# Expert outputs by way of DRAM rows for five of sixteen pairs, and three weight loads under way instead of two

## The chip, the cores and the metric

The program runs on one core of a Trainium2 chip. The metric is the device time of one execution in microseconds. The kernel before takes 706.75 us (median of three runs, 706.09 to 708.14). All engine names are those of the profile: PE is the matrix engine and PEld its weight loads, DVE, ACT and POOL are the vector, scalar and general engines, and SP only issues DMAs.

## The reference

One decoder layer on 512 tokens of width 1024, all in float32: RMSNorm, two attention branches with gates, an output projection, and then a mixture of experts with a final RMSNorm. What matters here is the mixture:

```python
g_sel = argmax(hf @ w_rg + b_rg)                  # one of 4 groups for each token
top_vals, top_idx = top_k(logits of the 8 experts in that group, 2)
weight = p_group * softmax(top_vals)
expert_id = g_sel * 8 + top_idx                    # two of 32 experts for each token
y[slot] = (silu(xs @ w_g[e]) * (xs @ w_u[e])) @ w_d[e]
out[token] += y[slot] * weight[slot]               # the sum of two slots for each token
```

The weights of each expert are three matrices of 1 MB, 96 MB for all 32, and every expert's weights are read once.

## The kernel before

The first 435 us hold the attention branches and the output projection. Each of those steps splits its operands in a high and a low part, and x2[0] to x2[3], four tiles of 128 tokens by 1024, hold the residual stream at their end. A router (class Route) then finds two experts for each token and its place among the tokens of that expert.

The experts are worked off in 16 pairs, q from 0 to 15, in `experts` (L819). A pair takes 128 slots, 64 for each of its two experts. One pair goes through these steps, in this order on PE:

- `gate_up` (L760): 32 matmuls G and 32 matmuls U (L769). ACT makes silu of G with the slots' norm factor (L774), DVE multiplies it with U (L775). The result is `a`.
- `some(5)`: five of the eight units of `combine` (L811) that the pair before has left. A unit is two matmuls of 128x512 (L815, L816) with a one-hot matrix S of slots against tokens, and one DVE addition to x2 (L817). There are 8 units in a pair: 4 token tiles by 2 halves of the width.
- `act_T` (L778): two transposes of `a` (L781) and a copy on ACT (L783).
- `some(3)`: the other three units.
- `next_rows`: eight transposes (L746) of the rows xg, which were gathered for the next pair.
- `down` (L786): 16 matmuls yp (L795), and for each half of the width a multiplication by the slots' weights sw on ACT (L802) and a low part on DVE (L803), both into the tile yhl. These are what the next pair's combine units multiply with S.

`gather_rows` (L723) is called at the end of pair q for pair q+2: two indirect DMAs on POOL fetch 128 rows of x2 (xg, from x2d) and of the routing weights (wg, from Wd). `slot_weights` (L733), three small copies on POOL at the top of each pair, makes sw and the norm factor out of wg.

PE and POOL keep the order in which the program states their work (`manual_schedule`, L826). The order on DVE, ACT and SP is the planner's. The pools that matter: mp has four PSUM buffers, which the combine units and the transposes share, yp has two, wg two, and xg, S, a and yhl one each.

The weights come in loads of 1 MB, 6 for each pair, all issued on SP by `load` (L678), which lets a load start when the load two before it has landed (L680, L681). There are NH = 20 buffers for them (`new_w`, L669), so a load also waits until the load 20 before it has been used. Pairs 0 to 2 are asked for ahead of the loop, pair q+2 at the top of pair q. The last pair's down weights come as four loads of 512 KB.

`last` (L876) is the combination of pair 15 and the final norm. The rows of x2 that leave the kernel take their additions from all pairs, so all combine units and the additions of the new way must be done before it ends.

Of the kernel before, what the change touches and what calls it, by code (L numbers as in the profile page):

```python
# [10 lines left out]
F32 = mybir.dt.float32  # L11
# [3 lines left out]
I32 = mybir.dt.int32  # L15
U32 = mybir.dt.uint32
AF = mybir.ActivationFunctionType
ALU = mybir.AluOpType
# [3 lines left out]
P = 128  # L22
T = 512
NT = T // P
D = 1024
# [5 lines left out]
NEG = -1e30  # L31
NE = 32
NH = 20


class Layer:
# [593 lines left out]
    def route_setup(self):  # L630
        nc, tc, io, c = self.nc, self.tc, self.io, self.const
        self.dram = dp = self.ctx.enter_context(tc.tile_pool(name="dram", bufs=1, space=bass.MemoryType.DRAM))
        self.x2d = dp.tile([T, D], F32, name="x2d")
        self.Wd = dp.tile([T, NE + 1], F32, name="Wd")
        self.wr = c.tile([P, KD, 40], F32, name="wr")
        nc.gpsimd.memset(self.wr, 0.0)
        self.load_late(self.wr[:, :, 0:4], io["w_router_group"][0].rearrange("(j p) g -> p j g", p=P))
        for g in range(4):
            self.load_late(self.wr[:, :, 8 + 8 * g:16 + 8 * g],
                              io["w_router_expert"][0, g].rearrange("(j p) e -> p j e", p=P))  # L640
        self.gpj = c.tile([P, KD], F32, name="gpj")
        self.load_late(self.gpj, io["ffn_norm"][0].rearrange("(p j) -> p j", p=P))
        self.gcol = gcol = c.tile([P, KD], F32, name="gcol")
        self.load_late(gcol, io["ffn_norm"][0].rearrange("(j p) -> p j", p=P))
        nc.vector.tensor_scalar(self.gpj, self.gpj, 32.0, None, ALU.mult)
        nc.vector.tensor_scalar(gcol, gcol, 32.0, None, ALU.mult)
        nc.vector.tensor_tensor(self.wr, self.wr, gcol.unsqueeze(2).to_broadcast([P, KD, 40]), ALU.mult)
        self.rb = c.tile([P, 40], F32, name="rb")
        nc.gpsimd.memset(self.rb, -3e38)
        self.load_late(self.rb[:, 0:4], io["b_router_group"][0:1, :].to_broadcast([P, 4]))  # L650
        self.load_late(self.rb[:, 8:40], io["b_router_expert"].rearrange("o g e -> o (g e)")
                          .to_broadcast([P, 32]))
        self.rc = c.tile([P, 33 + NT], F32, name="rc")
        self.load_late(self.rc, io["rconst"])
        self.iota32 = self.rc[:, 0:32]
        self.slot = self.rc[:, 32:33]
        self.token = self.rc[:, 33:33 + NT]
        self.tri = c.tile([P, 2, P], F16, name="tri")
        self.after(nc.gpsimd.dma_start(self.tri, io["tri"]), self.started)
        self.tm = c.tile([P, T], F16, name="tm")  # L660
        self.after(nc.gpsimd.dma_start(self.tm, io["tm"]), self.started)
        self.M = c.tile([P, NT, NE], F16, name="M")
        self.sq = c.tile([P, 2, NT], F32, name="sq")
        self.W = c.tile([P, NT, NE + 1], F32, name="W")
        self.iotaU = c.tile([P, NE], U32, name="iotaU")
        nc.vector.tensor_copy(self.iotaU, self.iota32)
# [10 lines left out]

    def load(self, dst, src):  # L678
        d = self.nc.sync.dma_start(dst, src)
        if len(self.loads) >= 2:  # L680
            self.after(d, self.loads[-2])  # L681
        self.loads.append(d)

    def load_w(self, src, how):
# [126 lines left out]
    def combine(self, S, y, half, t):  # L811
# [4 lines left out]
        nc.tensor.matmul(cp, S[:, t * P:(t + 1) * P], y[1], start=False, stop=True)  # L816
        nc.vector.tensor_tensor(self.x2[t][:, hs], self.x2[t][:, hs], cp, ALU.add)  # L817

    def experts(self):  # L819
        nc, tc = self.nc, self.tc  # L820
        NP = NE // 2
        wgu, wd = {}, {}
        for q in range(3):
            wgu[q], wd[q] = self.load_gu(q), self.load_d(q)
        self.yhl = self.wp.tile([P, 2048], F32R, name="yhl", tag="whi")
        with tc.manual_schedule(engines={mybir.EngineType.PE, mybir.EngineType.Pool}):  # L826
            xT, sw, xg = {0: self.xT0}, {}, {}
            S, y, todo = None, None, []
            for q in range(NP):
                if q > 0 and q + 2 < NP:  # L830
                    wgu[q + 2], wd[q + 2] = self.load_gu(q + 2), self.load_d(q + 2)
                    if q + 2 == NP - 1:
                        self.load_final()
                if q:
                    sw[q] = self.slot_weights(q, wg, nc.gpsimd)

                def some(n):
                    for _ in range(min(n, len(todo))):
                        self.combine(S, y[todo[0][0]], *todo[0])
                        todo.pop(0)  # L840

                def between(j):
                    if q == 0 and j == 3:
                        self.tokens()
                        xg[1] = self.gather_rows(self.xi[:, 1:2], self.rows)
                    if q == 0 and j == 5:
                        sw[0] = self.take_weights()
                    if q == 0 and j == 9:
                        self.count_blocks()
                a = self.gate_up(wgu.pop(q), xT.pop(q), lambda: sw[q][1], between)  # L850
                def next_rows():
                    xT[q + 1] = self.new_xT()
                    for g in range(2):
                        self.gathered_T(xg[q + 1][0], xT[q + 1], g)
                if q == 0:
                    next_rows()
                some(5)
                aT = self.act_T(*a)
                some(3)
                if 0 < q < NP - 1:  # L860
                    next_rows()
                if q + 1 < NP:
                    wg = xg.pop(q + 1)[1]
                if q + 2 < NP:
                    xg[q + 2] = self.gather_rows(self.xi[:, q + 2:q + 3])
                S = self.one_hot(self.xf[:, q:q + 1])
                dn = wd.pop(q)
                y = [None, None]
                todo = [(h, t) for h in range(2) for t in range(NT)]
                if q == NP - 1:  # L870
                    self.last(S, dn, aT, sw[q][0])
                    break
                for h in range(2):
                    y[h] = self.down(dn, aT, sw[q][0], h)
# [158 lines left out]
class Route:  # L1033
# [60 lines left out]
    def choose_experts(self):  # L1094
        nc, L = self.nc, self.L
        self.v8, vi = self.tmp("v8", [8]), self.tmp("vi", [8], U32)
        nc.vector.max(self.v8, self.es)
        nc.vector.max_index(vi, self.v8, self.es)
        self.Mk = self.tmp("Mk", [2, NE])
        nc.vector.tensor_tensor(self.Mk, L.iotaU.unsqueeze(1).to_broadcast([P, 2, NE]),  # L1100
                                vi[:, 0:2].unsqueeze(2).to_broadcast([P, 2, NE]), ALU.is_equal)
        nc.vector.tensor_tensor(L.M[:, self.t], self.Mk[:, 0], self.Mk[:, 1], ALU.add)
# [15 lines left out]

    def places(self):
        nc, L, t, N = self.nc, self.L, self.t, self.N  # L1120
        n = self.tmp("n", [2])
        for c in range(2):
            nc.vector.scalar_tensor_tensor(self.es, self.Mk[:, c], 1.0, N, ALU.mult, ALU.mult, accum_out=n[:, c:c + 1])
        self.at(self.AB[:, :, 0:64], n)
# [33 lines left out]
def shape_consts():  # L1158
    out = {}

    def tab(half):
        e = (-np.arange(half, dtype=np.float32) / np.float32(half)).astype(np.float32)
        inv = np.power(np.float32(500000.0), e).astype(np.float32)
        ang = np.arange(T, dtype=np.float32)[:, None] * inv[None, :]
        c, s = np.cos(ang).astype(np.float32), np.sin(ang).astype(np.float32)
        return [c, c, -s, s]
    out["rope"] = np.ascontiguousarray(np.concatenate(tab(16) + tab(8), axis=1))
    q = np.arange(P)[:, None]
    c = np.arange(T)[None, :]
    out["mask"] = np.where(c <= q + 384, np.float32(0), np.float32(NEG)).astype(np.float32)  # L1170
    tri = np.ones((P, 2, P), np.float32)
    tri[:, 0] = np.arange(P)[:, None] <= np.arange(P)[None, :]
    tri[:, 0] += 1024.0 * np.eye(P)
    out["tri"] = tri
    rc = np.zeros((P, 33 + NT), np.float32)
    rc[:, 0:32] = np.arange(32)
    rc[:, 32] = 1025 + np.arange(P) % 64
    rc[:, 33:] = np.arange(P)[:, None] + P * np.arange(NT)[None, :] - 1024
    out["rconst"] = rc
    out["tm"] = np.broadcast_to(np.arange(T, dtype=np.float32) - 1024, (P, T)).copy()  # L1180
    return out
# [30 lines left out]
```

## Time and profile before

| | us |
|---|---|
| median of three runs | 706.75 |
| the profiled execution's own time | 705.33 |
| its span | 703.5 |
| PE busy | 683.6 (97%) |
| DVE busy | 398.8 (57%) |
| ACT busy | 277.3 (39%) |
| POOL busy | 70.9 (10%) |

The span runs from the first to the last instruction. A row of the page's second part cuts it in 40 slices of 17.6 us, each digit being the busy share in tenths. Busy shares leave out DMA issues. An arrow in square brackets at a row's end names what ended the idle time ahead of it on its engine.

### The profile page before, as it was taken

Reading aid. Unit: us, or ns where it says so; the run is one execution under the profiler, and the core shown is the slowest. Engines: PE = TensorE matmul, PEld = TensorE weight load, DVE = VectorE, ACT = ScalarE, POOL = GpSimd, SP = SyncE. Lnnn points to the kernel's source line nnn. Section 1 sums busy time; section 2 is a strip of 40 time slices with the busy share of each in tenths; the row PEclk is TensorE's granted clock in tenths of the full one; section 3 lists DMA queues with packets and bytes.
Section 4 is the critical chain, followed back from the end, with each engine's and each line's share of the span. In section 5 each row is a group of like instructions: output and inputs, shape, how many; then the busy total and the mean of one; then the engine's idle time right before and its main releaser. Section 6 shows DMA issues by size and latency. Waiting matters only on the chain.

```text
span 703.5 us, 11377 instructions
## 1 busy us (share of the span) xinstructions
PE 683.6 (97%) x4262; PEld 522.5 (74%) x4262; DVE 398.8 (57%) x972; ACT 277.3 (39%) x623; POOL 70.9 (10%) x151
## 2 busy tenths in 40 slices
PE   8999999999999999999999999999999999999991
PEld 7998887777788888888888998566656666666651
DVE  5535956877829964423765317255555544555545
ACT  5747544555638663422333334211212111212123
POOL 1404000000000000000000012211121111111103
PEclk9999999999999999999999999999999999999996
DMA  8725431110272144212789758898999999999923
GB/s 256 152 61 90 106 121 60 61 49 13 68 171 61 27 156 119 61 61 94 262 301 352 287 189 315 316 361 308 377 364 393 392 394 355 372 377 348 367 89 122
DMA packets 73786, 148.17 MB, mean 211 GB/s; under 512 B 30938, under 2 KB 53554, under 8 KB 61952
## 3 DMA queue, kind: packets, MB, share of 16 engines
q1 hardware_dynamic: 67616, 138.69, 56.1%
q10 hardware_dynamic: 3040, 4.27, 2.3%
q0 software_dynamic: 3072, 4.46, 2.1%
q8 instruction: 35, 0.57, 0.3%
q14 instruction: 23, 0.19, 0.1%
HBM read 145.35 MB, written 4.26 MB: 213 GB/s over the span
## 4 chain that ended last, share of the span: by engine, by line
PE 88%; DMA 4%; issue 3%; DVE 2%; ACT 1%; POOL 1%; SPq 0%; POOLq 0%; DVEq 0%; ACTq 0%
PE yp L795 7%; PE G L769 6%; PE U L769 6%; PE pacc L96 5%; PE pacc L95 5%; PE pacc L94 5%; PE pacc L448 4%; PE pacc L447 4%; PE pacc L449 4%; PE cp L815 4%; PE cp L816 3%; PE ptr L420 3%; DMA wg<-Wd,xi 3%; PE S L402 2%; PE O L428 2%
## 5 line engine op out<-in xcount | busy, mean ns | idle before, releaser
L65 DVE SCALAR_TENSOR_TENSOR wlo<-wraw,ms,whi 128x256 fp32r<-128x256 f32 (+2 forms) x134 | 68.3, 552 | 31.4 <-ACT whi L64 31.2
L64 ACT ACTIVATE whi<-wraw,ms 128x256 fp32r<-128x256 f32 (+2 forms) x134 | 67.0, 559 | 42.1 <-PE pacc L448 20.1
L817 DVE TENSOR_TENSOR x<-x,cp 128x512 f32<-128x512 f32 x128 | 78.1, 682 | 0.8 <-PE cp L816 0.8
L94 PE MATMUL pacc<-whi,hThi 128*128 128x352 f32 (+1 forms) x192 | 72.6, 378 | 0.0
L95 PE MATMUL pacc<-wlo,hThi 128*128 128x352 f32 (+1 forms) x192 | 70.6, 369 | 0.0
L96 PE MATMUL pacc<-whi,hTlo 128*128 128x352 f32 (+1 forms) x192 | 70.5, 367 | 0.0
L775 DVE SCALAR_TENSOR_TENSOR a<-U,sw,a 128x256 f32<-128x256 f32 x16 | 11.0, 685 | 84.9 <-PE U L769 62.0
L795 PE MATMUL yp<-w,a 128*64 128x512 f32 x256 | 58.5, 598 | 0.5 <-ACT a L783 0.5
L769 PE MATMUL G<-w,xT 128*64 128x256 f32 x512 | 58.3, 380 | 0.0
L769 PE MATMUL U<-w,xT 128*64 128x256 f32 x512 | 58.2, 379 | 0.0
L769 PEld LDWEIGHTS G<-w,xT 128*64 128x64 f32 x512 | 36.5, 137 | 24.6 <-issue 4.6
L815 PE MATMUL cp<-yhl,S 128*128 128x512 f32 x128 | 53.6, 419 | 0.2 <-DVE x L817 0.2
L816 PE MATMUL cp<-yhl,S 128*128 128x512 f32 x128 | 50.8, 396 | 0.8 <-DVE yhl L803 0.8
L447 PE MATMUL pacc<-hThi,whi 128*128 128x512 f32 x128 | 50.6, 396 | 0.0
L448 PE MATMUL pacc<-hTlo,whi 128*128 128x512 f32 x128 | 50.4, 394 | 0.0
L769 PEld LDWEIGHTS U<-w,xT 128*64 128x64 f32 x512 | 36.7, 137 | 18.4
L449 PE MATMUL pacc<-hThi,wlo 128*128 128x512 f32 x128 | 50.1, 392 | 0.0
L415 ACT ACTIVATE E<-E,mx 128x128 f32<-128x128 f32 (+3 forms) x64 | 35.6, 557 | 20.5 <-DVE mx L412 19.7
L803 DVE SCALAR_TENSOR_TENSOR yhl<-yp,sw,yhl 128x512 fp32r<-128x512 f32 x32 | 24.0, 751 | 31.3 <-ACT yhl L802 31.3
L802 ACT ACTIVATE yhl<-yp,sw 128x512 fp32r<-128x512 f32 x32 | 22.0, 687 | 47.4 <-PE yp L795 47.4
L94 PEld LDWEIGHTS pacc<-whi,hThi 128*128 128x128 f32 x192 | 36.1, 188 | 5.2 <-issue 1.3
L95 PEld LDWEIGHTS pacc<-wlo,hThi 128*128 128x128 f32 x192 | 36.1, 188 | 4.5 <-issue 0.7
(221 smaller groups left out, 1307.8 us busy)
## 6 DMA issues: line engine op xcount, KB each, us to landing
w<-in_w_exp_gate_dram SPq DMA_DIRECT2D x32, 1024.0 KB, 6.1
w<-in_w_exp_up_dram SPq DMA_DIRECT2D x32, 1024.0 KB, 6.1
w<-in_w_exp_down_dram SPq DMA_DIRECT2D x30, 1024.0 KB, 5.8
wraw<-in_w_in_dram SPq DMA_DIRECT2D x14, 1024.0 KB, 5.3
wraw<-in_w_out_dram SPq DMA_DIRECT2D x4, 1024.0 KB, 7.1
wraw<-in_w_in_dram SPq DMA_DIRECT2D x5, 704.0 KB, 4.8
xs<-in_x_dram SPq DMA_DIRECT2D x4, 512.0 KB, 6.6
wraw<-in_w_o_mla_dram SPq DMA_DIRECT2D x4, 512.0 KB, 3.4
```

Source lines behind the costliest of these rows:

```text
L65: nc.vector.scalar_tensor_tensor(lo[:, k], raw[:, k], g, hi[:, k].bitcast(F32), ALU.mult, ALU.subtract)
L94: nc.tensor.matmul(ps[t][:, :ncols], act_hi[kk // 4][:, kk % 4, ts], hi[:, k], start=kk == 0, stop=False)
L95: nc.tensor.matmul(ps[t][:, :ncols], act_hi[kk // 4][:, kk % 4, ts], lo[:, k], start=False, stop=False)
L96: nc.tensor.matmul(ps[t][:, :ncols], act_lo[kk // 4][:, kk % 4, ts], hi[:, k], start=False, stop=kk == ktot - 1)
L447: nc.tensor.matmul(ps, hi[:, k, ds], self.hT[0][k // 4][:, k % 4], start=k == 0, stop=False)
L448: nc.tensor.matmul(ps, hi[:, k, ds], self.hT[1][k // 4][:, k % 4], start=False, stop=False)
L449: nc.tensor.matmul(ps, lo[:, k, ds], self.hT[0][k // 4][:, k % 4], start=False, stop=k == KD - 1)
L769: nc.tensor.matmul(GU[i][es, 0:256], xT[:, j, es], gu[e][i][:, j * 256:(j + 1) * 256], start=j == 0, stop=j == KD - 1)
L795: nc.tensor.matmul(yp[es], aT[:, j, es], wd[e][:, j * D + half * 512:j * D + half * 512 + 512], start=j == 0, stop=j == 1)
L815: nc.tensor.matmul(cp, S[:, t * P:(t + 1) * P], y[0], start=True, stop=False)
L816: nc.tensor.matmul(cp, S[:, t * P:(t + 1) * P], y[1], start=False, stop=True)
L817: nc.vector.tensor_tensor(self.x2[t][:, hs], self.x2[t][:, hs], cp, ALU.add)
```

## The change

For the pairs in VIA = (1, 3, 5, 7, 9), the slots' outputs are no longer combined by matmuls. `down_out` multiplies the two halves by sw on ACT into one tile y of 128x1024, and ACT issues a DMA that writes it to rows of a DRAM tensor yd (640 rows of 4 KB). In pairs 11 to 14, `take_slots` is called twice for token tile t = q - 11, once for each of a token's two choices: POOL clears a tile y, an indirect DMA on POOL fetches for each token the row yd[yi], where an index out of bounds fetches nothing, and DVE adds the tile to x2[t]. The indices yi are worked out in pair 1 (`slot_rows`) from the router's choices (Mk) and places (place), which are now kept, and from a constant row `base`.

The combine units of the pairs that are left are spread: in pairs 1 to 10 two units stand ahead of `act_T` and two behind it, so the eight units of pair 0, 2, 4, 6 and 8 last for two pairs. From pair 11 on it is five and three again, as before.

Thirdly, `load` waits for the load three before instead of two before.

```diff
+VIA = (1, 3, 5, 7, 9)
+        self.yd = dp.tile([len(VIA) * P, D], F32, name="yd")
...
     def load(self, dst, src):
         d = self.nc.sync.dma_start(dst, src)
-        if len(self.loads) >= 2:
-            self.after(d, self.loads[-2])
+        if len(self.loads) >= 3:
+            self.after(d, self.loads[-3])
...
+    def slot_rows(self):
+        nc, c = self.nc, self.const
+        rows = c.tile([P, NT, 2], F32, name="yrows")
+        far = c.tile([P, NT, 2], F32, name="far")
+        junk = c.tile([P, NE], F32, name="yjunk")
+        for t in range(NT):
+            for i in range(2):
+                nc.vector.scalar_tensor_tensor(junk, self.Mk[:, t, i], 1.0, self.base, ALU.mult, ALU.mult,
+                                               accum_out=rows[:, t, i:i + 1])
+        nc.vector.tensor_scalar(far, self.place, 1088.5, float(1 << 20), ALU.is_gt, ALU.mult)
+        nc.vector.tensor_tensor(rows, rows, self.place, ALU.add)
+        self.yi = c.tile([P, NT, 2], I32, name="yi")
+        nc.vector.tensor_tensor(self.yi, rows, far, ALU.add)
+
+    def down_out(self, wd, aT, sw, q):
+        nc = self.nc
+        y = self.bl.tile([P, D], F32, name="y", tag="yd", bufs=2)
+        for h in range(2):
+            nc.scalar.mul(y[:, h * 512:h * 512 + 512], self.down_products(wd, aT, h), sw)
+        i = VIA.index(q) * P
+        nc.scalar.dma_start(self.yd[i:i + P], y)
+
+    def take_slots(self, t, i):
+        nc = self.nc
+        y = self.bl.tile([P, D], F32, name="y", tag="yd", bufs=2)
+        nc.gpsimd.memset(y, 0.0)
+        nc.gpsimd.indirect_dma_start(out=y, out_offset=None, in_=self.yd,
+                                     in_offset=bass.IndirectOffsetOnAxis(ap=self.yi[:, t, i:i + 1], axis=0),
+                                     bounds_check=len(VIA) * P - 1, oob_is_err=False)
+        nc.vector.tensor_tensor(self.x2[t], self.x2[t], y, ALU.add)
...
-                some(5)
+                n = min(len(todo), 4) if VIA[0] <= q <= VIA[-1] + 1 else len(todo)
+                some((n + 1) // 2 + (n > 4))
                 aT = self.act_T(*a)
-                some(3)
+                some(n // 2 - (n > 4))
...
                 if q + 2 < NP:
                     xg[q + 2] = self.gather_rows(self.xi[:, q + 2:q + 3])
+                if q == 1:
+                    self.slot_rows()
+                if 0 <= q - VIA[-1] - 2 < NT:
+                    for i in range(2):
+                        self.take_slots(q - VIA[-1] - 2, i)
+                dn = wd.pop(q)
+                if q in VIA:
+                    self.down_out(dn, aT, sw[q][0], q)
+                    continue
                 S = self.one_hot(self.xf[:, q:q + 1])
-                dn = wd.pop(q)
```

The rest of the diff keeps Mk and place in tiles of their own and lengthens the constant rc by the 32 columns of `base`.

## Rows read from the trace of the kernel before

**Rows 1.** The page, its second part: busy tenths of the DMA engines and the rate of the DMAs, in 40 slices of the span.
```profile
DMA  8725431110272144212789758898999999999923
GB/s 256 152 61 90 106 121 60 61 49 13 68 171 61 27 156 119 61 61 94 262 301 352 287 189 315 316 361 308 377 364 393 392 394 355 372 377 348 367 89 122
```
**Rows 2.** What PE waited for from 435 us to the end, all of it: us in total, times, the longest.
```profile
PE yp L795 <- ACT a L783: 0.5, 1, 0.5
PE cp L816 <- DVE yhl L803: 0.8, 1, 0.8
PE cp L815 <- DVE x L817: 0.2, 1, 0.2
```
**Rows 3.** PE's instructions in order of time, of pair 2, the start of pairs 3 and 4 and the down products of pair 5: start, length, form, count. Of the units' matmuls, the second and third unit's first ones.
```profile
465.55 3.62 PE L769 MATMUL G<-w,xT 128*64 128x256 f32 x32
...
473.12 0.39 PE L815 MATMUL cp<-yhl,S 128*128 128x512 f32 x1
...
473.59 0.39 PE L815 MATMUL cp<-yhl,S 128*128 128x512 f32 x1
...
477.70 3.65 PE L795 MATMUL yp<-w,a 128*64 128x512 f32 x16
481.19 3.62 PE L769 MATMUL G<-w,xT 128*64 128x256 f32 x32
...
497.56 3.62 PE L769 MATMUL G<-w,xT 128*64 128x256 f32 x32
...
525.48 3.65 PE L795 MATMUL yp<-w,a 128*64 128x512 f32 x16
```
**Rows 4.** The same view, of pair 15: its gate and its down products.
```profile
669.86 3.62 PE L769 MATMUL G<-w,xT 128*64 128x256 f32 x32
...
681.02 3.65 PE L795 MATMUL yp<-w,a 128*64 128x512 f32 x16
```
**Rows 5.** SP's issues in order of time: start, time from the first issue's start to the last one's end, tile and source, count. The gate rows are those of pair 3, 4 and 15, the up and down rows at 440 and 447 us those of pair 3.
```profile
429.40 3.46 SPq L679 DMA_DIRECT2D w<-in_w_exp_gate_dram  x2
440.87 1.15 SPq L679 DMA_DIRECT2D w<-in_w_exp_up_dram  x2
447.23 3.29 SPq L679 DMA_DIRECT2D w<-in_w_exp_down_dram  x2
453.52 3.59 SPq L679 DMA_DIRECT2D w<-in_w_exp_gate_dram  x2
...
504.63 2.82 SPq L679 DMA_DIRECT2D w<-in_w_exp_down_dram  x2
509.63 2.83 SPq L679 DMA_DIRECT2D w<-in_w_exp_gate_dram  x2
...
651.30 2.82 SPq L679 DMA_DIRECT2D w<-in_w_exp_gate_dram  x2
...
669.33 0.55 SPq L679 DMA_DIRECT2D w<-in_w_exp_down_dram  x1
```
**Rows 6.** From the view of the tile w in the window from 669 to 670 us: the time from the last load's issue to its landing.
```profile
DMA to landing us min/median/max: 6.0/6.0/6.0
```
**Rows 7.** Busy time by windows; the last three columns are the granted clock of PE, the busy share of the 16 DMA engines and GB/s. The windows are a stretch without gathers, the stretch from gate 4 to the last up load, and the last 10.5 us of the loads.
```profile
504.63:514.66 10.03, 10.03 (x57) 6.12 (x58) 7.77 (x14) 2.67 (x6) 2.24 (x3) 1.00 1.01 408
...
453.50:664.80 211.30, 211.09 (x1428) 132.47 (x1425) 110.78 (x188) 41.26 (x80) 34.35 (x68) 1.00 0.96 369
664.80:675.30 10.50, 10.50 (x79) 6.11 (x79) 4.91 (x9) 3.58 (x6) 0.00 (x0) 1.00 0.68 229
```
**Rows 8.** The DMA view from 453 to 675 us: the queue of POOL's gathers with packets, MB and share of the engines' time, and the row gathers with their count and median us from issue to landing.
```profile
q0 software_dynamic: 2288, 3.66, 4.7%
...
xg<-x2d,xi POOLq DMA_INDIRECT x13, 6.9
```
**Rows 9.** POOL's instructions in order of time, end of pair 5 (gathers for pair 7) and the first two copies of pair 6; ahead of them a clearing of a 128x1024 tile, and the copy of pair 3, which waited longest.
```profile
429.26 0.95 POOL L619 MEMSET xg<- 128x1024 f32 x1
...
487.97 0.18 POOL L738 COPY sw<-wg 64x1 f32<-64x1 f32 x1 [7.38 <-DMA wg<-Wd,xi]
...
525.83 1.02 POOL L728 DMA_INDIRECT xg<-x2d,xi  x1 [6.81 <-PE ptr L746]
527.15 1.03 POOL L728 DMA_INDIRECT wg<-Wd,xi  x1 [0.30 <-issue]
528.17 0.20 POOL L738 COPY sw<-wg 64x1 f32<-64x1 f32 x1
533.08 0.18 POOL L738 COPY sw<-wg 64x1 f32<-64x1 f32 x1 [4.70 <-DMA wg<-Wd,xi]
```
**Rows 10.** ACT and DVE in order of time, in pair 6.
```profile
533.54 0.72 ACT L774 ACTIVATE a<-G,sw 128x256 f32<-128x256 f32 x1 [3.58 <-POOL sw L739]
...
536.17 0.68 DVE L775 SCALAR_TENSOR_TENSOR a<-U,sw,a 128x256 f32<-128x256 f32 x1 [5.43 <-PE U L769]
536.74 4.87 DVE L817 TENSOR_TENSOR x<-x,cp 128x512 f32<-128x512 f32 x8
```
**Rows 11.** What SP waited for over the whole span: us in total, times, the longest.
```profile
SPq L679 <- DMA w<-in_w_exp_gate_dram: 87.9, 28, 8.7
...
SPq L679 <- PE cp L816: 3.0, 12, 0.3
```
**Rows 12.** DVE in the tail: a two-input operation on a 128x1024 tile.
```profile
691.58 1.28 DVE L922 SCALAR_TENSOR_TENSOR fin<-x,rstd,fin 128x1024 f32<-128x1024 f32 x1 [0.58 <-POOL rstd L915]
```

More of the change, by code (lines that the diff above doesn't have):

```diff
@@ L652, in route_setup @@
                           .to_broadcast([P, 32]))
-        self.rc = c.tile([P, 33 + NT], F32, name="rc")
+        self.rc = c.tile([P, 33 + NT + NE], F32, name="rc")
         self.load_late(self.rc, io["rconst"])
@@ L657, in route_setup @@
         self.token = self.rc[:, 33:33 + NT]
+        self.base = self.rc[:, 33 + NT:]
         self.tri = c.tile([P, 2, P], F16, name="tri")
@@ L662, in route_setup @@
         self.M = c.tile([P, NT, NE], F16, name="M")
+        self.Mk = c.tile([P, NT, 2, NE], F32, name="Mk")
+        self.place = c.tile([P, NT, 2], F32, name="place")
         self.sq = c.tile([P, 2, NT], F32, name="sq")
@@ L1098, in choose_experts @@
         nc.vector.max_index(vi, self.v8, self.es)
-        self.Mk = self.tmp("Mk", [2, NE])
+        self.Mk = L.Mk[:, self.t]
         nc.vector.tensor_tensor(self.Mk, L.iotaU.unsqueeze(1).to_broadcast([P, 2, NE]),
@@ L1120, in places @@
         nc, L, t, N = self.nc, self.L, self.t, self.N
-        n = self.tmp("n", [2])
+        n = L.place[:, t]
         for c in range(2):
@@ L1174, in shape_consts @@
     out["tri"] = tri
-    rc = np.zeros((P, 33 + NT), np.float32)
+    rc = np.zeros((P, 33 + NT + NE), np.float32)
     rc[:, 0:32] = np.arange(32)
     rc[:, 32] = 1025 + np.arange(P) % 64
-    rc[:, 33:] = np.arange(P)[:, None] + P * np.arange(NT)[None, :] - 1024
+    rc[:, 33 + NT:] = [64 * (2 * VIA.index(i // 2) + i % 2) - 1025 if i // 2 in VIA else 1 << 20 for i in range(NE)]
+    rc[:, 33:33 + NT] = np.arange(P)[:, None] + P * np.arange(NT)[None, :] - 1024
     out["rconst"] = rc
```

## The prediction

> **What bounds the kernel now.** I read the page's slices first, then PE's waits, then PE in order of time, and SP's issues last. In the expert stage, from 435 us on, PE waits 1.5 us in all [rows 2]: PE sets the time. A pair takes it 481.19 - 465.55 = 15.64 us [rows 3]. Right behind PE stand the weights. From gate 4 to gate 15 the issues take 651.30 - 453.52 = 197.78 us for 11 pairs, 17.98 us a pair [rows 5], slower than PE. SP hardly waits there for a buffer (3.0 us for the units) but for earlier loads (87.9 us at the gate loads alone) [rows 11]. So the lead is eaten up: gate 4 is issued 497.56 - 453.52 = 44 us before PE uses it [rows 3, 5], gate 15 only 669.86 - 651.30 = 18.6 us [rows 4, 5]. The last load is issued at 669.33 and lands 6.0 us later, at 675.3 [rows 5, 6]. It holds the second half of the width, and PE comes to the second eight of the 16 down matmuls at 681.02 + 3.65/2, say 682.7 [rows 4]. **The slack is 7.4 us**: what is taken from PE beyond that buys nothing unless the loads also end earlier. The DMA engines run at 8 or 9 tenths in nearly every slice of this stage [rows 1].
>
> **PE's share.** Five pairs lose 16 combine matmuls each. A unit of two takes 473.59 - 473.12 = 0.47 us [rows 3], so 40 units are worth 40 x 0.467 = 18.7 us. That is the most that the change can give. Nothing is added on PE. DVE loses 40 additions of 0.61 us (4.87/8 [rows 10]), ten low parts and five one-hots, and gets eight additions of 128x1024, about 1.3 us each by the nearest two-input row [rows 12], and eleven small operations in pair 1. It is busy 57% and none of this is on the path, but for the place of the eight additions (below). ACT keeps its ten multiplications and gets five DMA issues. Spreading the units costs nothing by the rows: the multiplication of `a` starts at 536.17 and takes 0.68 [rows 10], and two units cover 0.93 us in place of 2.33. The cover is just enough, and anything that delays `a` now reaches PE at once.
>
> **POOL's queue.** The second copy of sw does not start when its own wg is there (the first copy runs at once, at 528.17); it starts at 533.08, when the gathers issued just ahead of it for the pair after next have landed [rows 9]. Then sw lets silu start at 533.54, which ends at 534.26, 1.9 us ahead of U's end at 536.17 [rows 10]. In pair 3 the copy came at 487.97 after 7.38 us of waiting instead of 4.70 [rows 9]; such a landing eats the 1.9 and more, with less cover. I take 2 us over pairs 2 to 11, between 0 and 6. Pairs 11 to 14 put two clearings (0.95 each) and two gathers (1.3 each with their gap, by 525.83 to 527.15) ahead of these copies [rows 9]: 4.5 us. If the copy waits for these too, in pair 12 to 14 it comes 4.5 us later; 1.9 are covered, and behind `a` on DVE stand the unit additions, which free PSUM for the next units. I take 2.7 to 4.4 a pair, 10.5 in all (in pair 15 the row gathers are absent, and it comes out even); at the least 0, if the copy doesn't wait for them. PE's own way then comes to the second half of the last down products at 682.7 - 18.7 + 2 + 10.5 = 676.5. In pairs that wait for weights anyway these waits lie beside each other.
>
> **The loads.** Four terms, all on the time of the last landing, 675.3.
> - Writes: 5 x 128 x 4 KB = 2.62 MB. At the rate of a stretch without gathers, 408 GB/s [rows 7], 6.4 us.
> - Gathered rows: of 1024 choices 5/16 fall on VIA pairs if the router spreads evenly (an estimate; 200 to 450), 320 x 4 KB = 1.31 MB, 3.2 us (2 to 4.5).
> - Disturbance: without gathers two loads take 509.63 - 504.63 = 5.0 us [rows 5], 15.0 a pair. The 17.98 hold 2.98 more. The gathers' bytes are 3.66 MB/13 = 0.28 MB or 0.69 us a pair [rows 8], idle engines 4% or 0.72 [rows 7], which leaves 1.57 us for each pair's gathers. The eight new ones may cost as much on top of their bytes (12.6 us) or nothing; they move two thirds as much, and I take 0.75 each, 6 us. For the writes, with no row of one beside the loads in this stage, the ends are the same, 0 to 1.57 each; I take 0, since every partition writes one whole row of 4 KB, while the gathers fetch some rows and skip others.
> - The third load: idle engine time is 4% of 211.3 = 8.5 us and 32% of the last 10.5 = 3.4 [rows 7], 11.9 in all. At the least it gives 0; at the most it also swallows the 13 x 1.57 = 20 us of disturbance. I take the idle time, 11.9, since an engine that is late through a gather can then hold back the others less. The step at 440 us, where up 3 waits for its buffer and down 3 then for a landing (447.23 [rows 5]), is inside this choice.
>
> Sum: 675.3 + 6.4 + 3.2 + 6 - 11.9 = 679.0. That is later than PE's 676.5, so **the loads set the end**, with a gain of 682.7 - 679.0 = 3.7 us. The profiled execution takes 705.33, so 701.6; the median of the runs shown is 1.4 above it, and **703.0** is forecast. The tail after the last down products is the same. From about pair 13 on PE would wait for weights.
>
> The loads ahead of 440 us may also start sooner by the third place. PE doesn't wait there for any load, and I cost this at nothing; what hides it is PE's work on the projections. If a weight of these came late behind an expert load, it would cost up to one load's time, 2.5 us.
>
> The Trainium skill speaks against the third load: DMA: Bandwidth & Descriptors, section "Where 436 GB/s comes from", says that HBM's share of about 358 GB/s for a core binds transfers from HBM to SBUF. By it 3.93 MB more would take 11.0 us and the third load would give nothing, 675.3 + 11.0 + 6 = 692.3 in place of 679.0, 716 in place of 703. The trace disagrees: 408 GB/s over ten microseconds with two loads under way, 369 over the whole stretch [rows 7].
>
> **The rivals.**
> - *The loads have nothing more to give.* Place: the 16 DMA engines in pairs 8 to 15. The engines are 0.96 busy, and if this is work, not waiting, then a third load only queues behind two. It decides from the point at which the additions exceed the third load's gain by 7.4 us. With 9.6 of bytes, 10 of disturbance and 4 of gain the last load lands at 690.9: 8.2 us slower, 715; in the middle of this case about 711. For it speaks the share of 1.01 in the fast stretch, with two loads under way; against it the 0.96 of the stretch and the 0.68 of the last 10.5 us [rows 7]. Chance 0.19. The Trainium skill's rule above would land in the same place.
> - *The loads get ahead.* The third load swallows part of the disturbance too, the last landing comes before 674, and PE with POOL's copies sets the end: 682.7 - 676.5 = 6.2 of gain, 700.5, and 697 where half of these copies' waits fail to come. For it: the stretch without gathers runs at 408 GB/s, the whole at 369 [rows 7], so what is lost hangs on the gathers. Without any such waits the full 18.7 would give 688. Chance 0.24 together.
> - *It does nothing that can be measured.* The bytes and the third load cancel, and the loads end 7.4 us later or a buffer is missing for a third load (against this: SP's waits [rows 11]). Then about 706.5. Chance 0.13.
> - The forecast, 700.5 to 705.5: chance 0.44.
>
> A measurement of this kernel tells about 0.3%, 2.1 us, from no change: faster is under 704.6, slower over 708.9. From the forecast's case 0.36 are faster and 0.08 the same; from the second rival all; from the third 0.01, 0.11 and 0.01; of the first 0.17 slower and 0.02 the same. Faster 0.61, same 0.21, slower 0.18. The range is 694 to 711: below it lies the case without POOL's waits, above it the worse half of the first rival. The likeliest case's own is 700.5 to 705.5.
>
> **What would show it.** PE's waits: right if from pair 12 or 13 on PE waits for loads of w, a few microseconds in all, and the pairs 2 to 10 take 13.8 us each. The units' matmuls L815 and L816 should be 88 each instead of 128. The second sw copy in pairs 12 to 14 should wait for the gather of y. SP's pace from gate 4 to gate 15 should be near 17.6 us a pair, and the DMA share 0.98 or more; at 18.5 the first rival holds, at 16.5 the second. The last load should land about 679. I am wrong in the main point if PE never waits for a load, or if the last load lands after 683.

## The result, and the profile after

The changed kernel takes 715.79 us (median of 4 runs, 714.57 to 716.87) beside 706.42 us of the kernel before: a ratio of 1.0132, 95% interval 1.0099 to 1.0165. It is slower; 703.0 was forecast, in a range of 694 to 711. The profiled execution's span is 715.0 us, against 703.5 before.

The page's slices of the kernel after, busy tenths, PE's granted clock and GB/s:
```profile
PE   8999999999999999999999999999999999686891
PEclk9999999999999999999999999999999999888996
DMA  8724431110361233213889667999999999999303
GB/s 251 142 69 87 107 119 59 60 60 1 82 154 59 61 119 117 79 40 114 270 282 384 231 238 268 404 414 413 406 414 416 363 398 384 415 400 384 121 1 121
```
What the reader is to see: from slice 26 on the DMAs move some 400 GB/s and fall off a slice earlier than before [rows 1], while PE, full until slice 34, has a hole in the slices 35 to 38, and its granted clock dips in the same place. PE's waits from 430 us to the end name the hole:
```profile
PE cp L820 <- DVE x L822: 18.1, 3, 7.8
PE G L786 <- DVE a L780: 2.3, 3, 0.9
PE cp L821 <- DVE yhl L808: 0.7, 1, 0.7
PE yp L800 <- ACT a L788: 0.5, 1, 0.5
```
Three waits of up to 7.8 us for the unit additions stand where before had one of 0.2 us [rows 2], and there is no wait for a load. The three lie in pairs 12, 13 and 14, each behind the fetch that is issued at the end of the pair ahead. Here is the same time on three engines, in pair 12, after the row and weight gathers for pair 13. PE, in order of time:
```profile
619.24 0.40 PE L821 MATMUL cp<-yhl,S 128*128 128x512 f32 x1
619.48 0.40 PE L820 MATMUL cp<-yhl,S 128*128 128x512 f32 x1
619.72 0.39 PE L821 MATMUL cp<-yhl,S 128*128 128x512 f32 x1
627.90 0.76 PE L820 MATMUL cp<-yhl,S 128*128 128x512 f32 x1 [7.79 <-DVE x L822]
...
630.17 0.63 PE L820 MATMUL cp<-yhl,S 128*128 128x512 f32 x1
630.60 0.63 PE L821 MATMUL cp<-yhl,S 128*128 128x512 f32 x1
```
POOL, the same view:
```profile
611.42 1.00 POOL L853 DMA_INDIRECT y<-yd,yi  x1 [0.27 <-POOL y L852]
...
613.66 1.00 POOL L853 DMA_INDIRECT y<-yd,yi  x1 [0.27 <-POOL y L852]
614.66 0.19 POOL L743 COPY sw<-wg 64x1 f32<-64x1 f32 x1
624.35 1.22 POOL L743 COPY sw<-wg 64x1 f32<-64x1 f32 x1 [9.49 <-DMA y<-yd,yi]
```
DVE, the same view:
```profile
621.00 1.23 DVE L856 TENSOR_TENSOR x<-x,y 128x1024 f32<-128x1024 f32 x1 [8.26 <-DMA y<-yd,yi]
624.29 1.23 DVE L856 TENSOR_TENSOR x<-x,y 128x1024 f32<-128x1024 f32 x1 [2.07 <-DMA y<-yd,yi]
626.58 0.66 DVE L780 SCALAR_TENSOR_TENSOR a<-U,sw,a 128x256 f32<-128x256 f32 x1 [1.06 <-ACT a L779]
627.09 3.05 DVE L822 TENSOR_TENSOR x<-x,cp 128x512 f32<-128x512 f32 x5
```
Two instructions stand at the head of their queues until the second fetch lands at 624.3: POOL's second copy of sw (without it no silu, no `a`), and DVE's additions of y, ahead of `a` and of the unit additions, which free the PSUM that PE wants. By these rows either alone would stop PE here; the experiments take them away one by one.

Behind the stall the units' matmuls follow one another at 630.60 - 630.17 = 0.43 us instead of 619.48 - 619.24 = 0.24. The windows (the last three columns are the granted clock, the DMA share and GB/s) show the granted clock beside it:
```profile
590.00:611.00 21.00, 21.00 (x137) 12.64 (x138) 12.35 (x22) 4.77 (x10) 5.46 (x8) 1.00 0.97 390
627.90:633.05 5.15, 5.15 (x19) 4.04 (x19) 4.30 (x7) 0.65 (x3) 0.00 (x0) 0.58 1.01 391
```
0.43 is the pace near the 1.2 GHz level (0.58 granted over these 5.15 us), 0.24 that at 2.4 GHz (1.00), and what went ahead is a PE that stood idle for 7.79 us. From 627.90 to the down products at 633.05 it takes 5.15 us where the same work took 607.48 - 604.32 = 3.16 a pair earlier: 2.0 us, and 1.6 and 1.5 behind the other two stalls.

From the start of the first gate matmul of a pair in PE's timeline, in us:
```
kernel                   pair 0   pairs 0-11   pairs 12-14   pair 15 to the end   span
before                   435.92     187.02         46.92           33.64          703.5
after                    440.58     170.39         70.57           33.46          715.0
```
So the change gave 16.6 us in pairs 0 to 11 and lost 23.65 in pairs 12 to 14 (18.1 of waits and 5.1 of lower clock are 23.2 of it), and 4.7 us were lost before the expert stage began.

The DMA view from 453 to 680 us, count, KB each and median us to landing, answers to [rows 8]:
```profile
w<-in_w_exp_gate_dram SPq DMA_DIRECT2D x24, 1024.0 KB, 8.1
yd<-y ACTq DMA_DIRECT2D x5, 512.0 KB, 8.3
xg<-x2d,xi POOLq DMA_INDIRECT x13, 8.6
y<-yd,yi POOLq DMA_INDIRECT x8, 8.3
```
Row gathers land in 8.6 us instead of 6.9. The last load is issued at 660.01 and lands 6.2 us later, at 666.2: 9 us earlier than before, with 3.9 MB more moved.

### The profile page after: what moved, and what is told of

The parts are those of the page before. It is cut to its first block, busy times and chain, and to the rows that moved or that the text cites. A ratio compares the mean times of both kernels' runs of the same rounds, so it can differ in the third digit from the quotient of the medians.

```text
span 715.0 us, 11091 instructions
## 1 busy us (share of the span) xinstructions
PE 675.1 (94%) x4182; PEld 512.6 (72%) x4182; DVE 377.0 (53%) x944; ACT 277.5 (39%) x623; POOL 90.3 (13%) x167
## 4 chain that ended last, share of the span: by engine, by line
PE 63%; DMA 19%; issue 9%; POOL 4%; DVE 2%; ACT 2%; POOLq 0%; SPq 0%; ACTq 0%; DVEq 0%
DMA wg<-Wd,xi 11%; PE pacc L96 5%; PE pacc L97 5%; PE pacc L95 5%; PE pacc L449 4%; PE pacc L448 4%; PE pacc L450 4%; DMA y<-yd,yi 4%; PE ptr L421 3%; PE S L403 2%; PE O L429 2%; PE pacc L492 2%; PE pacc L494 2%; PE pacc L473 2%; PE pacc L493 2%
## 5 line engine op out<-in xcount | busy, mean ns | idle before, releaser
L820 PE MATMUL cp<-yhl,S 128*128 128x512 f32 x88 | 40.9, 465 | 18.1 <-DVE x L822 18.1
L822 DVE TENSOR_TENSOR x<-x,cp 128x512 f32<-128x512 f32 x88 | 54.6, 678 | 2.3 <-PE cp L821 2.3
L779 ACT ACTIVATE a<-G,sw 128x256 f32<-128x256 f32 x16 | 11.4, 715 | 105.9 <-POOL sw L744 100.4
L449 PE MATMUL pacc<-hTlo,whi 128*128 128x512 f32 x128 | 51.0, 398 | 0.0
L97 PEld LDWEIGHTS pacc<-whi,hTlo 128*128 128x128 f32 x192 | 36.5, 190 | 4.2 <-issue 0.2
```

The source lines that it names most:

```text
L97: nc.tensor.matmul(ps[t][:, :ncols], act_lo[kk // 4][:, kk % 4, ts], hi[:, k], start=False, stop=kk == ktot - 1)
L449: nc.tensor.matmul(ps, hi[:, k, ds], self.hT[1][k // 4][:, k % 4], start=False, stop=False)
L820: nc.tensor.matmul(cp, S[:, t * P:(t + 1) * P], y[0], start=True, stop=False)
```

## The experiments

**The two waits.** Theory A: POOL's copy alone stops PE. B: DVE's queue alone. C: both, side by side, for the same landing. First the additions are made a pair later (`add_taken` is called ahead of the next `take_slots`, and waits for the pair's last unit addition), and POOL stays as it is:
```
     def take_slots(self, t, i):
...
-        nc.vector.tensor_tensor(self.x2[t], self.x2[t], y, ALU.add)
+        self.taken.append((t, y))
+
+    def add_taken(self):
+        for t, y in self.taken:
+            self.after(self.nc.vector.tensor_tensor(self.x2[t], self.x2[t], y, ALU.add), self.last_add)
+        self.taken = []
```


> The kernel after, with VectorE's additions of the fetched outputs (y) made one pair later, behind that pair's last unit addition; GpSimd's two copies of the weights stay as they are. In the trace after, two things of pairs 12 to 14 end at the landing of the same fetched rows: GpSimd's second copy (9.5, 8.7, 4.4, 2.2 us of wait) and VectorE's additions at the head of its queue (8.3 us in pair 12). Theory A, GpSimd's copy alone makes TensorE wait: the time stays at 714 to 717 us, and TensorE still waits some 18 us for VectorE's additions in pairs 12 to 14. Theory B, VectorE's queue alone: the 18.1 us of waits go, and most of the 5.1 us that the lower clock cost, so 690 to 695 us. Theory C, both wait for the same landing side by side: the activations a still wait for the copy, so 712 to 716 us, and the wait is then put down to a (G waiting for VectorE's a) rather than to the additions. A and C differ in the next run.

Measured: 714.72 us, ratio to before 1.0108 (1.0052 to 1.0164): 1.1 us less than after, within what can be told apart. B is out. PE's waits, and DVE in pair 12:
```profile
PE cp L820 <- DVE x L822: 14.3, 3, 6.7
PE G L786 <- DVE a L780: 2.3, 3, 0.8
```
```profile
625.68 0.66 DVE L780 SCALAR_TENSOR_TENSOR a<-U,sw,a 128x256 f32<-128x256 f32 x1 [12.75 <-ACT a L779]
626.19 3.06 DVE L822 TENSOR_TENSOR x<-x,cp 128x512 f32<-128x512 f32 x5
```
C had the label of the wait wrong: it is still put down to the unit additions. But DVE's row says why: at its head now stands `a`, which waits for ACT, which waits for POOL's copy, and the unit additions stand behind `a`. One releaser is named, and the cause is two engines further.

Then the copies. Two multiplications over all partitions with 0/1 columns take the place of the copies into the halves, and the additions stay:
```
-        for e in range(2):
-            es = slice(64 * e, 64 * e + 64)
-            eng.tensor_copy(sw[es, 0:1], wg[es, 2 * q + e:2 * q + e + 1])
+            for e in range(2):
+                eng.tensor_tensor(sw[:, e:e + 1], wg[:, 2 * q + e:2 * q + e + 1], self.half01[:, e:e + 1], ALU.mult)
+            eng.tensor_tensor(sw[:, 0:1], sw[:, 0:1], sw[:, 1:2], ALU.add)
```


> The kernel after, with GpSimd's two copies into halves of the partitions replaced by two multiplications over all 128 partitions with columns of 0 and 1 and an addition; VectorE's additions stay in place. Theory A, GpSimd's copy alone: the 18.1 us of TensorE's waits and most of the 5.1 us of lower clock go, 690 to 695 us. Theory B, VectorE's queue alone: 714 to 717 us. Theory C, both side by side: 712 to 717 us, TensorE's wait for VectorE's additions still 14 to 18 us, while GpSimd's weights are ready some 8 us earlier in pairs 12 to 14.

Measured: 706.23 us, ratio 0.9996 (0.9968 to 1.0024), 9.6 us less than after. POOL makes its weights right behind the gathers of y (the second is issued at 608.06), with no wait. Its row, PE's wait, and DVE's from 600 us on:
```profile
609.09 0.33 POOL L744 TENSOR_TENSOR sw<-wg,rc 128x1 f32<-128x1 f32 x2
```
```profile
PE cp L826 <- DVE x L828: 12.6, 3, 6.1
```
```profile
DVE x L862 <- DMA y<-yd,yi: 23.6, 6, 7.7
```
A is out: DVE alone still costs PE 12.6 us. C's 712 to 717 is missed too, from below. By the pairs' starts in the profiled executions (table below; their spans differ by 12.3 us, 1.5 of it ahead of pair 0) 6.7 of the gain lie in pairs 12 to 14, and 4.1 in pairs 0 to 11, which C had left out: there the second copy had been waiting for the next row and weight gathers. Over the whole stage of the kernel after, the second copy waits 76.6 us for these in 11 pairs and 24.7 for y in four; the operations over all partitions have no such wait. Why a copy that begins in the second half of the partitions waits for gathers that it doesn't read, while operations over all partitions don't, is not shown.

Both edits:

> The kernel after, with both edits. Theory C (and whichever of A and B holds): no wait of TensorE for the fetched rows is left, 18.1 us of waits and some 5.1 us of lower clock go, and a little of the 2.3 us of waits for a, so 715.8 - 25 = about 691 us, 688 to 695. If it stays above 705, the wait comes from something else than these two consumers of the fetched rows (the buffers of the additions, or the loads).

Measured: 689.09 us, ratio 0.9754 (0.9692 to 0.9815), 26.7 less than after. All that PE still waits for:
```profile
PE cp L827 <- DVE yhl L814: 1.1, 1, 1.1
PE yp L806 <- ACT a L794: 0.5, 1, 0.5
```
C holds: alone the edits give 1.1 and 9.6, together 26.7. Last, another way to free the copies: their form stays, the additions are late, and the gathers of y are issued behind the copies of the next pair's weights.
```
                     sw[q] = self.slot_weights(q, wg, nc.gpsimd)
+                if 0 <= q - VIA[-1] - 3 < NT:
+                    for i in range(2):
+                        self.take_slots(q - VIA[-1] - 3, i)
```


> The kernel after with the additions one pair later, as in the first run, and with the gathers of y issued one place later on GpSimd: behind the copies of the next pair's weights instead of ahead of them. GpSimd's copies keep their form. If what holds the second copy is only that the gathers are issued ahead of it (theory C): 688 to 692 us, as with both edits. If the form of the copy itself waits for whatever gather is under way, also one issued behind it, or if the later fetch comes too late for the last additions: 700 us or more.

Measured: 698.17 us, ratio 0.9872 (0.9813 to 0.9931): between the two expectations, 17.6 less than after and 9.1 more than with both edits. POOL in pair 12:
```profile
608.48 0.20 POOL L743 COPY sw<-wg 64x1 f32<-64x1 f32 x1
615.54 0.18 POOL L743 COPY sw<-wg 64x1 f32<-64x1 f32 x1 [6.86 <-DMA wg<-Wd,xi]
...
617.20 1.03 POOL L853 DMA_INDIRECT y<-yd,yi  x1 [0.27 <-DMA w<-in_w_exp_gate_dram]
```
The copy waits for what is issued ahead of it: y no longer, but still the row and weight gathers of the next pair. So the place on POOL's queue decides, and the first half of the expectation named only one of the two things ahead. The pairs, as in the table above:
```
kernel                   pair 0   pairs 0-11   pairs 12-14   pair 15 to the end   span
additions late           440.31     170.84         66.64           34.21          712.0
copies                   439.07     166.31         63.86           33.46          702.7
both                     439.06     166.31         46.91           34.42          686.7
gathers of y later       439.17     170.10         50.24           34.09          693.6
```
With both, pairs 12 to 14 take what they took before, and pairs 0 to 11 are 187.02 - 166.31 = 20.7 us shorter.

**The third load.** On the kernel before, alone:
```
-        if len(self.loads) >= 2:
-            self.after(d, self.loads[-2])
+        if len(self.loads) >= 3:
+            self.after(d, self.loads[-3])
```


> The kernel before with the third load of weights alone. In the kernel before TensorE's own way sets the end and the loads had 7.4 us to spare, so an earlier last load should give nothing: 704.5 to 707.5 us, with the last load landing some 10 us earlier than before's 675.3 us, 400 to 417 GB/s where before had some 369. Rival: three loads under way lengthen the landing of GpSimd's gathers (6.9 us before, 8.6 after), which TensorE then meets in the weights of a pair: 708 to 712 us.

Measured: 706.90 us, ratio 0.9995 (0.994 to 1.005). As expected in the time, and not in the size: the last load, here issued at 643.82,
```profile
w<-in_w_exp_down_dram SPq DMA_DIRECT2D x1, 512.0 KB, 5.4
```
lands at 649.2, 26.1 us earlier than before's 675.3, not 10. Then the reverse, two loads in the kernel after and in the one with both edits:

> The kernel after with two loads under way instead of three. Theory: the third load is what stretched the landing of the fetched rows (8.3 us by the issues' median, some 10.5 us in pair 12), so with two loads they land some 2 us earlier, TensorE's waits in pairs 12 to 14 fall from 18 to some 12 us, and the time to 708 to 713 us, unless TensorE now waits for loads. Rival, the gathers' landing does not hang on the third load: waits stay at 17 to 19 us and the time at 715 to 718 us.

> Both edits of the run before, with two loads under way. By the prediction's sum the third load brings the last landing 11.9 us forward; if so, with two the loads set the end: TensorE waits for the last pairs' weights, and the time is 697 to 703 us against 689 with three. Rival: two loads keep up with TensorE, 688 to 691 us, and the third was not needed.

Measured: 731.55 us (1.0361, 1.0287 to 1.0435) and 730.72 (1.0334, 1.0268 to 1.04). Both theories on the first fall in the time, the first by the case that it excepted (PE now waits for loads), and 697 to 703 on the second falls too, in the size. The waits for the fetched rows do shrink, in the first, from 18.1 to 3.8 us, but the loads now set the end, in the second too:
```profile
PE U L774 <- DMA w<-in_w_exp_up_dram: 18.6, 10, 3.2
PE G L774 <- DMA w<-in_w_exp_gate_dram: 5.9, 4, 2.1
PE cp L820 <- DVE x L822: 3.8, 2, 1.9
```
```profile
PE U L780 <- DMA w<-in_w_exp_up_dram: 19.0, 11, 3.5
PE G L780 <- DMA w<-in_w_exp_gate_dram: 4.9, 3, 3.1
```
With both edits the third load is worth 730.72 - 689.09 = 41.6 us. One window, 453.5 to 643 us, of before, before with three loads, both edits with two, and both edits, in this order:
```profile
453.50:643.00 189.50, 189.28 (x1284) 118.24 (x1282) 99.11 (x168) 37.18 (x73) 31.26 (x60) 1.00 0.97 370
```
```profile
453.50:643.00 189.50, 189.08 (x1266) 116.02 (x1264) 98.79 (x168) 37.08 (x72) 31.26 (x60) 1.00 1.01 411
```
```profile
453.50:643.00 189.50, 175.37 (x1180) 105.42 (x1178) 66.06 (x111) 36.11 (x71) 35.10 (x71) 0.97 0.95 348
```
```profile
453.50:643.00 189.50, 189.50 (x1356) 116.19 (x1354) 80.38 (x132) 41.35 (x80) 49.01 (x90) 1.00 1.01 409
```
With two loads the rate falls from 370 to 348 GB/s when the writes and fetches come; with three it stays at 409 to 411, and the extra bytes cost little more than their own time (3.9 MB at 409 GB/s are 9.6 us; the last landing moves by 11.6, below). The Trainium skill (HBM Reference, "Specifications (TRN2)") says that a core alone draws about 425 GB/s, bounded by its 16 DMA engines, well above the share of 358; these rows agree with that, and not with the 358 that the forecast weighed.

**Ahead of the expert stage.** PE's instructions and its waits up to pair 0 are those of before, and still it comes 4.7 us later. What differs is where buffers lie: by the tiles' sizes, the larger constants push the big ones 544 bytes on. Theory D says that this place sets the pace; in the kernel before:
```
+        c.tile([P, 8], F32, name="pad")
```


> The kernel before with one unused 32-byte tile among the constants, which moves the buffers behind it by 32 bytes in SBUF and nothing else. In the trace after, TensorE begins the expert stage 4.7 us later than before, with the same instructions and waits up to there, and its matmuls of the router and of the mixing follow one another at 0.233 instead of 0.229 us; these buffers lie 544 bytes further. Theory D, the place of the moving operand sets that pace: 709 to 711 us, with the same 0.233 us pitch. Rival, what the loads do earlier or a difference between executions makes it: 705 to 707.5 us, the pitch stays 0.229.

Measured: 709.26 us, ratio 1.0054 (1.0018 to 1.0091), 3.1 us more. Theory D holds, as far as the buffers' place goes; which operand's place counts is not shown, since the pad moves all the buffers behind it. The windows of the gates' projections (`gate_T`, L447 to L449 in before, which the expectations call the router) and of the mixing, of before and with the 32 bytes; the second column is PE's busy time and matmuls:
```profile
257.00:330.00 73.00, 73.00 (x321) 59.89 (x320) 27.50 (x58) 26.93 (x58) 0.00 (x0) 1.00 0.29 90
330.00:375.00 45.00, 45.00 (x198) 36.87 (x197) 31.91 (x54) 16.12 (x31) 0.00 (x0) 1.00 0.84 288
```
```profile
257.00:330.00 73.00, 73.00 (x314) 58.72 (x314) 26.31 (x57) 25.61 (x56) 0.00 (x0) 1.00 0.30 93
330.00:375.00 45.00, 45.00 (x195) 36.20 (x194) 30.89 (x53) 15.72 (x32) 0.00 (x0) 1.00 0.77 262
```
321 against 314 matmuls in the same 73 us, 0.227 against 0.232 us each by these counts, at a granted clock of 1.00 in both. The starts in PE's timeline agree: nine matmuls take 2.06 us before (258.57 to 260.63) and 2.10 with the pad (258.69 to 260.79), 0.229 against 0.233 each. Two more pads in the kernel with both edits, of 32 and of 480 bytes (the buffers then lie 576 and 1,024 bytes on from their place before):

> Both edits, and the unused 32 bytes among the constants that bring the buffers behind them back to before's place within 64 bytes. Theory D (the moving operand's place sets 0.233 against 0.229 us a matmul): 689.1 - 3.2 = 685.9 us, 684.5 to 687.5, and the expert stage begins at 436 us as before, not at 439. Rival, what the pad did to the kernel before was chance: 688 to 690 us.

> Both edits, with 480 unused bytes among the constants: the large buffers then lie 1,024 bytes behind their place in the kernel before (544 bytes in the kernel after and with both edits, 576 with the 32 bytes). If the place within some power of two up to 1,024 bytes decides (theory D, more widely): the router and the mixing run at 0.229 us a matmul again, the expert stage begins at 436 us instead of 439.1, and the time is 689.1 - 3.2 = 686 us. Rival, the place does not matter or matters by something else than the distance: 0.233 us, 438 to 439 us, 688 to 690 us.

Measured: 687.98 us (0.9729, 0.9675 to 0.9782) and 685.59 (0.969, 0.9647 to 0.9734). With 32 bytes it gained 1.1 us, pair 0 began at 438.3, and the rival came nearer, so the place within 64 bytes isn't the measure. With 1,024 the forecast of D came true to 0.4 us: the first gate matmuls, of both edits' run with 480 bytes,
```profile
L781 PE MATMUL G<-w,xT x32: 379/379/430, 435.9 to 440.5; 128*64 128x256 f32 x32
```
begin at 435.9 as before (439.1 without the pad). Which distances below 1,024 would do is open; 0 and 1,024 were fast, 32 and 544 slow, 576 hardly better. This is the fastest kernel of the study.

The other 1.5 of the 4.7 us lie in the first 15 us: four transposes that start at 7.8 us take 1.08 us in the executions of after, of after with two loads and of the late additions, 0.63 in those of before, of the copies' edit and of both edits. From 7.5 to 13 us PE does 28 matmuls in after and 39 in before, at a granted clock of 1.00 in both. What decides it wasn't tried.

**What bounds it then.** Seven pairs through DRAM, on the fastest kernel:
```
-VIA = (1, 3, 5, 7, 9)
+VIA = (1, 3, 5, 6, 7, 8, 9)
```


> The run with 480 bytes, with seven pairs through DRAM (1, 3, 5, 6, 7, 8, 9) instead of five. The fetch stays at eight gathers; 16 units of two matmuls go, 16 x 0.467 = 7.5 us of TensorE, and two writes of 512 KB come. Theory E, TensorE's own way still sets the end with both edits: 7 to 8 us less than the run with five pairs (678 to 679 where that one is 686). Rival, the loads are near to setting it (410 GB/s from 453 us on): the last load lands no earlier, two writes later by 2.6 us in all, and the gain is 0 to 4 us.

Measured: 690.29 us (0.9767, 0.972 to 0.9815), 4.7 more than with five. E falls, and the rival was too kind. PE's waits:
```profile
PE U L781 <- DMA w<-in_w_exp_up_dram: 4.2, 4, 2.0
PE G L793 <- DVE a L787: 3.4, 4, 0.8
PE cp L828 <- DVE yhl L815: 1.1, 1, 1.1
PE G L781 <- DMA w<-in_w_exp_gate_dram: 0.9, 1, 0.9
```
PE has less to do and waits more, for loads (5.1 us) and for `a`, whose cover the removed units were (3.4). Here PE meets the loads with three of them under way too.

## Why the prediction was wrong

**PE's share, 18.7 us: right.** The units' matmuls are 88 each instead of 128, and with both edits pairs 0 to 11 are 20.7 us shorter. Of the 2 us beyond, 0.9 lay in pairs 3 and 4 of before, which took 16.37 and 15.77 us in place of 15.64; most of the rest is that a pair with four units fewer takes 13.67 us with both edits, 1.97 less than 15.64 and not 4 x 0.467 = 1.87.

**POOL's waits: the step that failed.** The mechanism was named (the copy waits for what is issued ahead of it, y included) and sized at 2 us for pairs 2 to 11 and 10.5 for pairs 12 to 14. Measured were 4.1 (the copies' edit) and 23.65, DVE's part with it. "In pair 12 to 14 it comes 4.5 us later" counted the time to issue the clearings and gathers and took the landing as it was: the copy came when the second y landed, 10.6 us after its issue (613.66 to 624.29), by 9.5 us of waiting. That is 13.4 us behind the pair's first gate matmul (610.97), where pair 6 of before had 4.1 (528.97 to 533.08): 9.3 us later, not 4.5. And a stall was priced at its own length; each cost some 1.7 us more at the lower clock.

**DVE's additions: "none of this is on the path, but for the place of the eight additions"** was the second failure. The place was excepted and never priced. They stood at the head of DVE's queue, ahead of `a`. Since both blocks end at one landing, the waits name only one of them, and neither edit alone shows the gain of both.

**The loads: wrong in the main point**, as the prediction said it would be if PE never waits for a load. The last landing came at 666.2, not 679.0, at a pace of SP's gate loads of (643.02 - 454.77)/11 = 17.1 us a pair, between the forecast's 17.6 and the 16.5 of the second rival. The bytes and the disturbance came out at three quarters of their size for three loads: on the kernels whose pair 0 starts at 436, from 649.2 (before with three) to 660.8 (both edits with 480 bytes: the last load issued at 654.22 and 6.6 us under way) it is 11.6 us, against 15.6 in the sum. The third load was mis-sized: 11.9 taken, 26.1 measured without the extra traffic; the upper end of 31.9 held it. And the terms don't add: with two loads the same traffic moves the last landing from 675.3 to 707.2 (702.79 and 4.4 us), 3.1 us of which are the later start, so 28.8 instead of 11.6.

**The sum of it.** The spans were to be 703.5 - 3.7 = 699.8 us and the profiled execution has 715.0, 15.2 more: 13.15 in pairs 12 to 14 (23.65 against 10.5), 2.1 in pairs 0 to 11 (4.1 against 2), and 4.7 ahead of pair 0, for which the sum had no term; less the 2.0 of PE's share, the 2.5 by which the loads were to end behind PE, and 0.2 in the tail.

**The rivals.** The first (the loads have nothing more to give) gave the right time, 715, for a wrong reason. The second had the right place (the loads get ahead, POOL's copies set the end), and its 688 without such waits is what both edits reached; its 700.5 with them was short by the step above. (Its 697 for half of these waits doesn't follow: half of 2 + 10.5 us would give 694.3.) The loads ahead of 440 us, costed at nothing, were not what delayed PE there: with the third load alone, before begins pair 0 at 436.01, 0.1 us later.

## What to carry to other kernels

An instruction moved onto a queue costs what stands behind it, not its own length: for a DMA fetch, name every engine that waits for the landing, take the landing as it will be with the new traffic, and ask what is queued behind each waiter; when two wait for one landing, only removing both shows the gain. Loads limited by how many may be under way are not a fixed bandwidth: find out first, with that limit alone changed, what the engines can do. A stall of PE cost more here than its own length (1.5 to 2.0 us more behind each), so compare the pace and the granted clock behind it too.

## What was not expected of the hardware

- An unused tile of 32 bytes costs 3.1 us of 706: the matmuls of the gates' projections and of the mixing take some 2% longer each (0.233 instead of 0.229 us), with nothing changed but the buffers' place.
- A third load of 1 MB under way, alone in the kernel before, takes the DMAs from 370 to 411 GB/s and the median landing of a row gather from 6.9 to 8.6 us; both are worth knowing before such a limit is raised.
- POOL's copy of 64x1 took 1.22 us beside DVE's addition of 1.23 that began 0.06 us ahead of it, and 0.18 in the run in which the addition was a pair later. The Trainium skill (SBUF — State Buffer, "Who interferes with whom") says that a VectorE instruction with two SBUF inputs contends with a GpSimd one that reads SBUF; the rows agree.
